# Experts by wide weight tiles, with 128 stationary columns and the second bias taken by gates

## The chip, the cores and the metric

One core of a Trainium2 chip runs the whole program: TensorE (PE, with its weight loads PEld), VectorE (DVE), ScalarE (ACT), GpSimd (POOL), SyncE (SP, which only issues DMAs here) and 16 DMA engines. The metric is device time in microseconds of one execution; before and after are compared by the median of runs.

## The reference, cut to what matters

Two transformer blocks over 512 tokens of width 1024. The change is in the mixture of experts that ends the first block: 32 experts, four for each token, so 64 tokens an expert on average.

```
logits = xt @ router_w + router_b
top_logit, top_idx = top_k(logits, 4)
gate = softmax(top_logit)
for each expert e, for the tokens that chose it:
    hid = x @ w1[e] + b1[e]                    # w1: 1024 x 2048
    glu = min(hid[:, :1024], 7)
    lin = clip(hid[:, 1024:], -7, 7)
    act = glu * sigmoid(1.702 * glu) * (lin + 1)
    y   = (act @ w2[e] + b2[e]) * gate         # w2: 1024 x 1024
out = x + gate2 * (sum of y over a token's experts)
```

All is fp32. The weights of the experts are 384 MiB, each read once.

## The kernel before, in words

**Products.** Each factor is cut into a high part (fp32r, a cast on ACT, L104) and a low part (a subtraction on DVE, L105), and a product is three matmuls: high x high, high x low, low x high (`mm3`, L98). For the experts the activations are stationary (96 places an expert, `CAP`) and the weights move, 512 columns a matmul.

**Weight tiles.** A tile of weights is 512 rows x 512 columns, 1 MiB, as [128, 4, 512]; an expert has twelve, eight of the first layer (L1) and four of the second (L2). `weights` (L968) writes the order: L1 of expert e, then L2 of expert e-1; at the end L1(30), L2(29), L2(30), L1(31), L2(31). SP loads tiles into eight raw buffers (`load`, L982); a load is issued when the tile that had its buffer is cut. The high and low parts have four buffers of a tile each, used by halves (`PB=2`: a cast and a subtraction for each half tile of 1024 elements a partition). `ahead` is 3: in step n of the loop the code issues the cut of tile n+3 (`split`), then the products of tile n, then whatever `plan` has hung behind step n (`after`). PE, ACT, DVE and SP keep this written order; each runs its own queue in order. GpSimd's order is the scheduler's.

**An expert.** With b the step of its first tile, `plan` (L1093) hangs: gather of the next expert's tokens (POOL, `gather` L1050) behind b; their transposes on PE (`turn` L1056) behind b+6 and the cut of these into xt (`parts` L1063: a copy on ACT, a subtraction on DVE, for each half of 384 elements) behind b+8. The hidden columns come as half 0 of gate and linear part (tiles b to b+3), then half 1. `swiglu` (L1071) runs behind b+4 and b+8 for 512 columns each: a min (DVE L1073), a silu (ACT), a clip (DVE L1076), a gating (DVE L1077). The gated rows (ln) are turned and cut into `at` behind b+11 to b+14. L2 of the expert begins at b+20; behind its last tile `finish` (L1137) multiplies y by gate and gate2 (ys, DVE L1134) and GpSimd adds the rows to `acc` in DRAM by a scatter (L1225).

**Biases.** b1 and b2 of all experts are held as high and low parts (`b1s`, `b2s`), cut in the first steps (`bias_split`, `BS`). A matmul with a one-hot column `e2` adds them: four for L1 and two for L2 of each expert.

**Around it.** `phase_r` (L748) makes the first residual, the router and the lists; `route` (L826) does a block of 128 tokens, with the gates in the tile B. `EARLY` tiles of weights are cut there with GpSimd doing the subtraction, and the third at the beginning of `phase_b`. The last expert isn't scattered: its rows (`last`, L1126) are put back by a one-hot matmul (`onehot`) while x gets `acc` by a DMA at step `SM` (L1180). Then `overflow` (a loop that usually runs no pass) and the norm of the second block.

Of the kernel before, what the change touches and what calls it, by code (L numbers as in the profile page):

```python
# [18 lines left out]
T = 512  # L19
# [15 lines left out]
SM = 378  # L35
YH = 2
F30 = 3
XN = 12
L30 = [8,8,9,9,10]
TS = 1  # L40
GO = 0
NG = 2
TQ = [("tr",2),("y",2)]
# [4 lines left out]
PB = 2  # L48
# [3 lines left out]
MB = dict(xg=1,xt=1,at=1,gl=2,ln=2,ys=1,raw=7,hl=4)  # L52
# [3 lines left out]
BS = [0,2,4,6,8,10]  # L56
LS = [7,5,6,8,9]
# [5 lines left out]
class Ker:  # L63
# [684 lines left out]
    def phase_r(self, RY, yH, yL):  # L748
# [10 lines left out]
        rowi = self.rowi = lp.tile([128, NT, 4], I32, name="rowi")  # L759
        self.ovr = lp.tile([1, 359], I32, name="ovr")  # L760
# [65 lines left out]
        def route(i, lg):  # L826
# [141 lines left out]
    def weights(self):  # L968

        L1 = lambda e: [(e, 1, hb, m, kh) for hb in range(2) for m in range(2) for kh in range(2)]  # L970
        L2 = lambda e: [(e, 2, kh, cb, 0) for kh in range(2) for cb in range(2)]
        seq = self.seq = []
        for e in range(NE):
            seq += L1(e) + (L2(e - 1) if e else [])
            if e == NE - 2:
                seq += L2(e)
        del seq[-4:]
        seq += L2(NE - 1)
        self.at_ = {c: n for n, c in enumerate(seq)}
        self.raw, self.hl = {}, {}  # L980

    def load(self, n):  # L982
        if n < len(self.seq):
            e, layer, u, v, kh = self.seq[n]
            if layer == 1:
                src = self.a["exp_w1"][0][e, 512 * kh:512 * kh + 512, 512 * u + D * v:512 * u + D * v + 512]
            else:
                src = self.a["exp_w2"][0][e, 512 * u:512 * u + 512, 512 * v:512 * v + 512]
            two = n % RAW >= self.nraw
            w = self.raw[n] = (self.wp2 if two else self.wp).tile([128, 4, 512], F32, name="wraw", tag="wraw",  # L990
                                                                  bufs=RAW - self.nraw if two else self.nraw)
            self.nc.sync.dma_start(w, src.rearrange("(k p) c -> p k c", p=128))
# [10 lines left out]
    def phase_b(self):  # L1003
# [8 lines left out]
        b2s = bb.tile([128, D], F32R, name="b2s")  # L1012
# [3 lines left out]
        for t in (b1s, b2s, e2):  # L1016
            nc.gpsimd.memset(t[64:128].bitcast(F32), 0.0)
# [4 lines left out]
        psum = self.pool(PS, "psb", space=PSUM)  # L1022
        P = lambda tag, bufs: psum.tile([128, 512], F32, name=tag, tag=tag, bufs=bufs)
        T_ = lambda tag, n=512: bp.tile([C, n], F32, name=tag, tag=tag, bufs=MB[tag])

        braw = {}

        def bias_load():
            for n, (src, c0, tag, w) in enumerate((("exp_b1", 0, "gl", 512), ("exp_b1", D, "gl", 512), ("exp_b1", 512, "ln", 512),
                                                   ("exp_b1", D + 512, "ln", 512), ("exp_b2", 0, "ys", 1024))):  # L1030
                t = T_(tag, w)
                for h in range(2):
                    nc.sync.dma_start(t[32 * h:32 * h + 32], a[src][0, :, c0:c0 + w])
                braw[n] = t, (b1s if n < 4 else b2s)[:, c0:c0 + w]
# [6 lines left out]
        def gate_rows():  # L1041
            for j in range(2):
                p = P("tr", 2)
                mm(p, self.ones[32 * j + 64:32 * j + 65, :], self.mod[2][32 * j + 64:32 * j + 65, :])
                nc.scalar.copy(g2[:, 512 * j:512 * j + 512], p[:C])
# [10 lines left out]
        def turn(src, b, c0):  # L1056

            p = P("tr", 2)
            for k in range(4):
                nc.tensor.transpose(p[:, k * C:(k + 1) * C], src[:, c0 + k * 128:c0 + (k + 1) * 128], self.ident[:C, :C])  # L1060
            return p[:, 0:4 * C].rearrange("p (k c) -> p k c", c=C), slice(4 * b, 4 * b + 4)

        def parts(t, dst, scale=1.0):  # L1063
            pv, ks = t
            self.act(dst[0][:, ks, :], pv, AF.Copy, scale=scale)
            nc.vector.scalar_tensor_tensor(dst[1][:, ks, :], pv, scale, dst[0][:, ks, :].bitcast(F32), op0=OP.mult, op1=OP.subtract)  # L1066
# [4 lines left out]
        def swiglu(pg, pl):  # L1071
            gl = T_("gl")
            nc.vector.tensor_scalar(gl, pg[:C], 7.0, None, op0=OP.min)  # L1073
# [4 lines left out]
            return ln  # L1078
# [14 lines left out]
        def plan(e):  # L1093

            b, y0 = at_[(e, 1, 0, 0, 0)], at_[(e, 2, 0, 0, 0)]
            if e + 1 < NE:
                after(b, keep(("xg", e + 1), lambda: gather(e + 1)))
                n = b + XN if e == NE - 2 else b + 6
                for q in range(2):
                    after(n, keep(("tx", e + 1, q), lambda q=q: turn(X["xg", e + 1], q, 512 * q)))  # L1100
                after(n + 1 if e == NE - 2 else max(min(at_[e + 1, 1, 0, 0, 0], b + 12) - ahead - 1, b + 7),
                      lambda: (X.__setitem__(("xt", e + 1), pair("at" if e == NE - 2 else "xt")),
                               [parts(X["tx", e + 1, q], X["xt", e + 1]) for q in range(2)]))
            steps = LS if e == NE - 1 else L30 if e == NE - 2 else (8, 11, 12, 13, 14)
            after(b + 4, keep(("ln", 0), lambda: swiglu(*X["hid", e, 0])))
            after(b + steps[0], keep(("ln", 1), lambda: swiglu(*X["hid", e, 1])))
            for q in range(2):
                after(b + steps[1 + 2 * q], keep(("t", q), lambda q=q: turn(X["ln", q], q, 0)))
                after(b + steps[2 + 2 * q], lambda q=q: (q or X.__setitem__(("at", e), pair("xt" if e >= NE - 2 else "at")),
                                                         parts(X["t", q], X["at", e], 1 / 1.702)))  # L1110
            if e < NE - 1:
                after(y0 + (F30 if e == NE - 2 else 4), lambda: finish(e))
            else:
                after(y0 + OH, onehot)
                for cb in range(2):
                    after(y0 + LA + cb, lambda cb=cb: last(cb))

        def onehot():

            io, t = T_("gl"), bp.tile([C, 1], F32, name="tlc")  # L1120
# [5 lines left out]
        def last(cb):  # L1126
            if cb == 0:
                X["ys"] = self.wp.tile([C, 4, 512], F32R, name="ysp", tag="wraw", bufs=self.nraw)
            ys = T_("ln")
            weigh(ys, NE - 1, cb)  # L1130
            self.split(X["ys"][:, cb], X["ys"][:, 2 + cb], ys)

        def weigh(ys, e, cb):
            nc.vector.scalar_tensor_tensor(ys, X["y", e][cb][:C], self.tlg[:, e:e + 1], g2[:, 512 * cb:512 * cb + 512],  # L1134
                                           op0=OP.mult, op1=OP.mult)

        def finish(e):  # L1137
            ys = T_("xg" if e == NE - 2 else "ys", D)
            for cb in range(2):
                weigh(ys[:, 512 * cb:512 * cb + 512], e, cb)  # L1140
            self.add_rows(ys, self.tli[:, e:e + 1])

        def products(n):
            e, layer, u, v, kh = seq[n]
            if layer == 1:
                if u == 0 and v == 0 and kh == 0:
                    plan(e)
                if v == 0 and kh == 0:
                    X["hid", e, u] = [P("hid", 4), P("hid", 4)]
                p, xt, bias = X["hid", e, u][v], X["xt", e], b1s[:, D * v + 512 * u:D * v + 512 * u + 512]  # L1150
            else:
                if u == 0 and v == 0:
                    X["y", e] = [P("hid", 4) if e >= NE - YH else P("y", 2) for _ in range(2)]
                p, xt, kh, bias = X["y", e][v], X["at", e], u, b2s[:, 512 * v:512 * v + 512]
            w = hl.pop(n)
            for k in range(4):
                kk = 4 * kh + k
                self.mm3(p[:C], (xt[0][:, kk, :], xt[1][:, kk, :]), w[k], kk == 0, False)
            if kh:
                mm(p[:C], e2[:, e:e + 1].to_broadcast([128, C]), bias, False, True)  # L1160

        ET_ = mybir.EngineType
        with self.tc.manual_schedule(engines={ET_.PE, ET_.Activation, ET_.DVE, ET_.SP}):
# [3 lines left out]
            for n in range(5):  # L1167
                after(BS[n], lambda n=n: bias_split(n))
            after(BS[5], gate_rows)
# [3 lines left out]
            for q in range(2):  # L1173
                parts(turn(X["xg", 0], q, 512 * q), X["xt", 0])
# [15 lines left out]
        ES.close()  # L1190
        self.overflow(P)
# [36 lines left out]
    def overflow(self, P):  # L1228
# [8 lines left out]
        with tc.For_i(0, n, 1) as b:  # L1237
# [27 lines left out]
            b1, b2 = (a[n_][0][bass.ds(e, 1), :] for n_ in ("exp_b1", "exp_b2"))  # L1265

            def gemm(xt, w, c0, bias):
                p = P("hid", 4)
                bb = op_.tile([1, 512], F32, name="bb", bufs=2)
# [561 lines left out]
```

## Time and profile before

| | us |
|---|---|
| runs of the kernel before, median of 3 | 2538.77 (2535.23 to 2539.68) |
| the profiled execution | 2528.63 |
| its span | 2526.8 |
| PE, DVE, ACT, POOL busy in it | 2432.6, 1837.4, 1378.7, 389.9 |
| PE matmuls into hid and y by lines, of 4512 | 1571.8 |
| DVE subtractions `wl` (L105), x974 | 1080.6 |

The profile is of one execution. Its times are microseconds from the start of the span; a name is a line of the kernel, an engine, an operation and the tiles written and read. Busy time counts overlapping instructions once, so the start-to-start distance of instructions in a row can be smaller than their duration. The experts run from about 531 to 1692 us, the second block after them.

### The profile page before, as it was taken

The page shows a single profiled execution, that of the slowest core. Times are in us where ns is not written, and L with a number is a line of the kernel's source. Part 1 is how long each engine was busy: PE and PEld are TensorE (multiplying, and loading weights), DVE is VectorE, ACT ScalarE, POOL GpSimd, SP SyncE. Part 2 cuts the span into 40 slices and gives each one's busy share as a digit, 9 for nine tenths or more (in the row PEclk, how much of TensorE's full clock was granted, in tenths as well). Part 3 has the DMA queues.
Part 4 walks back from the last instruction along what each step waited for, and adds up shares of the span by engine and source line. Part 5 has one row for each costly group of instructions (what it writes and reads, how often), then busy time and mean ns, then how long its engine had stood idle before and what let it go on. Part 6 is the DMA issues. An engine that isn't in the chain of part 4 may idle for free. (4 is left out here: it accounts for less than half of the span.)

```text
span 2526.8 us, 33228 instructions
## 1 busy us (share of the span) xinstructions
PE 2432.6 (96%) x12362; PEld 1785.6 (71%) x12362; DVE 1837.4 (73%) x2627; ACT 1378.7 (55%) x1956; POOL 389.9 (15%) x319
## 2 busy tenths in 40 slices
PE   6999998979999999999999999998999999899999
PEld 2677764756777777777777777667877678688887
DVE  3445566689999999999999999986765544555522
ACT  2433455357777777777777777764445543332221
POOL 2000223214221333233210111130100000000000
PEclk7999799989999999999999999998999999899999
DMA  9462100679999999999999999983411131433331
GB/s 277 151 199 67 50 1 30 231 250 337 349 375 370 369 374 375 371 370 369 367 368 366 369 373 372 373 250 103 94 51 42 43 89 63 119 96 99 93 100 67
DMA packets 371566, 556.75 MB, mean 220 GB/s; under 512 B 13138, under 2 KB 153501, under 8 KB 371401
## 3 DMA queue, kind: packets, MB, share of 16 engines
q1 hardware_dynamic: 359808, 518.81, 59.1%
q0 software_dynamic: 11120, 34.68, 6.0%
q8 instruction: 98, 1.61, 0.3%
q10 hardware_dynamic: 473, 1.11, 0.1%
q14 instruction: 67, 0.55, 0.1%
HBM read 534.06 MB, written 20.48 MB: 219 GB/s over the span
## 5 line engine op out<-in xcount | busy, mean ns | idle before, releaser
L105 DVE TENSOR_TENSOR wl<-wraw,wh 128x1024 fp32r<-128x1024 f32 (+2 forms) x974 | 1080.6, 1157 | 253.2 <-ACT wh L104 239.7
L104 ACT CAST wh<-wraw 128x1024 fp32r<-128x1024 f32 (+1 forms) x980 | 942.2, 998 | 542.8 <-PE mm L96 236.4
L96 PE MATMUL hid<-wh,xt 128*96 128x512 f32 x2048 | 671.4, 396 | 0.6 <-DVE xt L1066 0.5
L96 PEld LDWEIGHTS hid<-wh,xt 128*96 128x96 f32 x2048 | 331.5, 162 | 138.0 <-DVE xt L1066 1.2
L96 PE MATMUL hid<-wl,xt 128*96 128x512 f32 x1024 | 402.0, 393 | 0.0
L96 PE MATMUL y<-wh,at 128*96 128x512 f32 x960 | 310.0, 393 | 0.0
L1225 POOL DMA_INDIRECT acc<-ys,tli x30 | 190.6, 6353 | 545.1 <-DVE ys L1134 525.5
L96 PE MATMUL mm<-hH,wh 128*128 128x512 f32 x624 | 253.4, 407 | 3.3 <-ACT gate L1600 1.9
L96 PE MATMUL mm<-hL,wh 128*128 128x512 f32 x624 | 248.9, 399 | 0.0
L96 PE MATMUL mm<-hH,wl 128*128 128x512 f32 x624 | 248.7, 399 | 0.0
L96 PEld LDWEIGHTS hid<-wl,xt 128*96 128x96 f32 x1024 | 166.1, 162 | 63.9 <-issue 0.3
L96 PEld LDWEIGHTS y<-wh,at 128*96 128x96 f32 x960 | 155.4, 162 | 66.8
L96 PE MATMUL y<-wl,at 128*96 128x512 f32 x480 | 188.4, 393 | 0.0
L96 PEld LDWEIGHTS mm<-hH,wh 128*128 128x128 f32 x624 | 118.6, 190 | 37.3 <-issue 5.7
L96 PEld LDWEIGHTS mm<-hL,wh 128*128 128x128 f32 x624 | 118.4, 190 | 28.2 <-issue 3.8
L96 PEld LDWEIGHTS mm<-hH,wl 128*128 128x128 f32 x624 | 118.5, 190 | 27.1 <-issue 2.6
L74 ACT ACTIVATE gl<-gl 96x512 f32<-96x512 f32 x64 | 40.5, 632 | 156.9 <-DVE gl L1073 156.9
L96 PEld LDWEIGHTS y<-wl,at 128*96 128x96 f32 x480 | 77.6, 162 | 32.8
L1052 POOL DMA_INDIRECT xg<-h2d,tli x32 | 45.8, 1431 | 292.9 <-PE tr L1060 285.6
L96 PE MATMUL mu<-hH,wh 128*128 128x512 f32 x176 | 68.5, 389 | 0.0
L96 PE MATMUL mu<-hL,wh 128*128 128x512 f32 x176 | 68.5, 389 | 0.0
L96 PE MATMUL mu<-hH,wl 128*128 128x512 f32 x176 | 68.5, 389 | 0.0
(558 smaller groups left out, 3361.8 us busy)
## 6 DMA issues: line engine op xcount, KB each, us to landing
wraw<-in_exp_w_dram SPq DMA_DIRECT2D x384, 1024.0 KB
wraw<-in_w_in_dram SPq DMA_DIRECT2D x62, 512.0 KB
wraw<-in_ada_w_dram SPq DMA_DIRECT2D x48, 512.0 KB
wraw<-in_w_ffn_in_dram SPq DMA_DIRECT2D x44, 512.0 KB
wraw<-in_w_ffn_out_dram SPq DMA_DIRECT2D x22, 512.0 KB
wraw<-in_w_out_dram SPq DMA_DIRECT2D x4, 1024.0 KB
wraw<-in_w_o_dram SPq DMA_DIRECT2D x8, 512.0 KB
acc<-zf SPq DMA_DIRECT2D x1, 2432.0 KB
```

The lines of the kernel that those rows point to most:

```text
L74: ins = self.nc.scalar.activation(out, in_, func, **kw)
L96: self.nc.tensor.matmul(out, l, r, start=start, stop=stop, skip_group_check=True)
L104: self.nc.scalar.copy(h, src)
L105: (eng or self.nc.vector).tensor_sub(l, src, h.bitcast(F32))
L1052: self.gathered = nc.gpsimd.indirect_dma_start(out=xg, out_offset=None, in_=self.h2d, in_offset=bass.IndirectOffsetOnAxis(ap=self.tli[:, e ...
L1225: self.nc.gpsimd.indirect_dma_start(out=self.acc, out_offset=bass.IndirectOffsetOnAxis(ap=idx, axis=0), in_=ys, in_offset=None, compute_op ...
```

## The change

- A tile of an expert below 30 (`OLD`) becomes 256 rows x 1024 columns, [128, 2, 1024]; a tile of L1 is then wholly of the gate or of the linear part. Experts 30 and 31 keep the old tiles. Parts are cut by whole tiles (`PB=1`), 2048 elements a partition.
- The stationary factors xt and at have 128 columns, the last 32 zeroed once; the matmuls write all 128 rows.
- SwiGLU, the cuts of xt and at, ys and their PSUM tiles (`P2`, two banks) go by whole 1024 columns: min and silu behind b+4, clip behind b+8, gating behind b+9, turn behind b+11, cut of at behind b+12, cut of the next xt behind b+7.
- b2 leaves the products. The gates of each token by expert, G, are summed in `route` on GpSimd; b2 times gate2 is cut into `b3`, and in the last sums (x += one-hot @ rows) one more matmul adds G-turned @ b3.
- The gather leaves out places of index 512 and above (`bounds_check`); xg is zeroed once.
- At the end L2(30) comes between the halves of L1(31); `SM`, `LS`, `L30` and `BS` are moved.

```diff
-SM = 378
+SM = 379
-L30 = [8,8,9,9,10]
+L30 = [8,10,12,12,13]
+OLD = 30
-PB = 2
+PB = 1
-MB = dict(xg=1,xt=1,at=1,gl=2,ln=2,ys=1,raw=7,hl=4)
+MB = dict(xg=1,xt=1,at=1,gl=1,ln=1,ys=1)
-BS = [0,2,4,6,8,10]
-LS = [7,5,6,8,9]
+BS = [0,1,10,14]
+LS = [11,7,8,12,13]
...
+            nc.gpsimd.tensor_add(G[:, i, :], B[:, 0, NE:], B[:, 1, NE:])
+            for j in range(2, 4):
+                nc.gpsimd.tensor_add(G[:, i, :], G[:, i, :], B[:, j, NE:])
...
-            seq += L1(e) + (L2(e - 1) if e else [])
-            if e == NE - 2:
-                seq += L2(e)
-        del seq[-4:]
+            l1, l2 = L1(e), L2(e - 1) if e else []
+
+            seq += l1[:4] + l2 + l1[4:] if e == NE - 1 else l1 + l2
         seq += L2(NE - 1)
...
+            w = self.a["exp_w1" if layer == 1 else "exp_w2"][0][e]
+            if e < OLD:
+                v, kq = divmod(i, 4)
+                src, shape = w[256 * kq:256 * kq + 256, D * v:D * v + D], [128, 2, D]
...
+        def gated_bias():
+
+            t, _ = braw.pop(2)
+            nc.vector.tensor_mul(t, t, g2)
+            nc.scalar.copy(b3, t)
+            nc.vector.tensor_sub(b3[32:64], t[32:64], b3[32:64].bitcast(F32))
+
+        def turned_gates():
+
+            gb = X["gb"] = self.wp.tile([96, D + T], F32R, name="gb", tag="wraw", bufs=self.nraw)
+            G3 = self.wp.tile([128, 96 * NT], F32, name="G3", tag="wraw", bufs=self.nraw)
+            p, GT = P2("tr")[:, 0], gb[:, D:]
+            nc.gpsimd.tensor_copy(G3.rearrange("p (i r e) -> p i r e", r=3, e=NE), self.G.unsqueeze(2).to_broadcast([128, NT, 3, NE]))
+            nc.gpsimd.tensor_copy(gb[:, 0:D], b3)
+            for i in range(NT):
+                nc.tensor.transpose(p[:96, 128 * i:128 * i + 128], G3[:, 96 * i:96 * i + 96], self.ident)
+            nc.scalar.copy(GT, p[:96])
+            nc.vector.tensor_sub(GT[64:96], p[64:96], GT[64:96].bitcast(F32))
...
-            xg = T_("xg", D)
+            xg = T_("xg")
+            if e == 0:
+                nc.gpsimd.memset(xg, 0.0)
+
             self.gathered = nc.gpsimd.indirect_dma_start(out=xg, out_offset=None, in_=self.h2d,
-                                         in_offset=bass.IndirectOffsetOnAxis(ap=self.tli[:, e:e + 1], axis=0))
+                                         in_offset=bass.IndirectOffsetOnAxis(ap=self.tli[:, e:e + 1], axis=0),
+                                         bounds_check=T - 1, oob_is_err=False)
...
-            return [bp.tile([128, KD, 128], F32R, name=f"{name}{j}", bufs=MB[name])[:, :, 0:C] for j in range(2)]
+
+            if name not in X:
+                X[name] = [bp.tile([128, KD, 128], F32R, name=f"{name}{j}") for j in range(2)]
+                for t in X[name]:
+                    nc.gpsimd.memset(t[:, :, C:].bitcast(F32), 0.0)
+            return X[name]
...
+        def glu(gl, pg):
+            nc.vector.tensor_scalar(gl, flat(pg), 7.0, None, op0=OP.min)
             self.act(gl, gl, AF.Silu, scale=1.702)
-            ln = T_("ln")
-            nc.vector.tensor_scalar(ln, pl[:C], 7.0, -7.0, op0=OP.min, op1=OP.max)
+
+        def lin(ln, pl):
+            nc.vector.tensor_scalar(ln, flat(pl), 7.0, -7.0, op0=OP.min, op1=OP.max)
+
+        def gated(ln, gl):
             self.last = nc.vector.scalar_tensor_tensor(ln, ln, 1.0, gl, op0=OP.add, op1=OP.mult)
...
+                after(b + 6, keep(("tx", e + 1), lambda: turn(X["xg", e + 1], P2("tr"), 0, 2)))
+                after(b + 7,
+                      lambda: (X.__setitem__(("xt", e + 1), pair("xt")),
+                               parts(X["tx", e + 1], X["xt", e + 1], 0, 2)))
+            if e < OLD:
+                after(b + 4, lambda: (X.__setitem__("gl", T_("gl")), glu(X["gl"], X["hid", e, 0])))
+                after(b + 8, lambda: (X.__setitem__("ln", T_("ln")), lin(X["ln"], X["hid", e, 1])))
+                after(b + 9, lambda: gated(X["ln"], X["gl"]))
+                after(b + 11, keep("t", lambda: turn(X["ln"], P2("tr"), 0, 2)))
+                after(b + 12, lambda: (X.__setitem__(("at", e), pair("at")), parts(X["t"], X["at", e], 0, 2, 1 / 1.702)))
...
+            if e < OLD:
+
+                v, kq = divmod(i, 4)
+                todo_ = [(2 * kq + k, j, [t[:, 512 * j:512 * j + 512] for t in w[k]], D * v + 512 * j)
+                         for k in range(2) for j in range(2)]
...
+            for kk, j, wk, c0 in todo_:
+                self.mm3(p[:, j], (xt[0][:, kk, :], xt[1][:, kk, :]), wk, kk == 0, kk == KD - 1 and b0 is None)
+                if kk == KD - 1 and b0 is not None:
+                    mm(p[:C, j], e2[:, e:e + 1].to_broadcast([e2.shape[0], C]), b0[:, c0:c0 + 512], False, True)
...
+                mm(p, X["gb"][:, D + 128 * i:D + 128 * i + 128], X["gb"][:, cs], True, False)
                 for j in range(2):
-                    mm(p, X["one"][:, 128 * i:128 * i + 128], X["ys"][:, 2 * j + cb], j == 0, j == 1)
+                    mm(p, X["one"][:, 128 * i:128 * i + 128], X["ys"][:, 2 * j + cb], False, j == 1)
```

## Rows read from the trace of the kernel before

**Rows 1.** A stretch of the expert stage: length, engines' busy time (instructions), clock, DMA share, GB/s.

```profile
820.00:1590.00 770.00, 770.00 (x3565) 546.45 (x3564) 737.85 (x769) 569.73 (x640) 181.35 (x44) 1.00 1.05 370
```

**Rows 2.** Timeline of GpSimd: start, duration, line, operation; gathers (xg) and scatters (acc).

```profile
655.89 1.15 POOL L1052 DMA_INDIRECT xg<-h2d,tli  x1 [6.50 <-PE tr L1060]
...
1249.31 2.63 POOL L1225 DMA_INDIRECT acc<-ys,tli  x1 [17.74 <-DVE ys L1134]
...
1576.85 6.35 POOL L1225 DMA_INDIRECT acc<-ys,tli  x1 [22.52 <-DVE ys L1134]
1588.94 1.92 POOL L1052 DMA_INDIRECT xg<-h2d,tli  x1 [5.74 <-PE tr L1060]
```

**Rows 3.** Timeline of PE among the experts, and the chain's piece of the final projection.

```profile
999.83 0.62 PE L96 MATMUL hid<-wh,xt 128*96 128x512 f32 x2
...
1009.73 0.62 PE L96 MATMUL hid<-wh,xt 128*96 128x512 f32 x2
...
2402.43 119.69 PE ro L96 x528
```

**Rows 4.** Timeline of DVE over one expert while it catches up.

```profile
699.15 1.02 DVE L1066 SCALAR_TENSOR_TENSOR xt<-tr,xt 128x384 fp32r<-128x384 f32 x2
700.09 0.68 DVE L1073 TENSOR_SCALAR gl<-hid 96x512 f32<-96x512 f32 x1
700.68 0.68 DVE L1076 TENSOR_SCALAR ln<-hid 96x512 f32<-96x512 f32 x1
...
702.40 9.17 DVE L105 TENSOR_TENSOR wl<-wraw,wh 128x1024 fp32r<-128x1024 f32 x8 [0.25 <-ACT wh L104]
711.49 1.40 DVE L1134 SCALAR_TENSOR_TENSOR ys<-y,tlg,g2b 96x512 f32<-96x512 f32 x2
712.82 0.54 DVE L1066 SCALAR_TENSOR_TENSOR at<-tr,at 128x384 fp32r<-128x384 f32 x1
...
734.23 1.01 DVE L1066 SCALAR_TENSOR_TENSOR xt<-tr,xt 128x384 fp32r<-128x384 f32 x2
```

**Rows 5.** Waits, us in total, times, longest: 900 to 1300, then 1250 to 1600.

```profile
ACT wh L104 <- DMA wraw<-in_exp_w_dram: 8.9, 15, 1.4
...
ACT wh L104 <- DMA wraw<-in_exp_w_dram: 40.5, 68, 1.7
```

**Rows 6.** DMA totals of two stretches of 2 us: 458 to 460, then 452 to 454.

```profile
DMA packets 391, 0.77 MB, mean 385 GB/s; under 512 B 15, under 2 KB 15, under 8 KB 391
...
DMA packets 200, 0.82 MB, mean 412 GB/s; under 512 B 0, under 2 KB 0, under 8 KB 199
```

**Rows 7.** Forms of splits on DVE and ACT (xcount, busy, mean ns), and ACT beside a SwiGLU.

```profile
L105 DVE TENSOR_TENSOR wl<-wraw,wh 128x1024 fp32r<-128x1024 f32 x862 | 1005.1, 1219 | 174.6 <-ACT wh L104 161.4 <-PE st L96 8.5 <-issue 0.2
...
L105 DVE TENSOR_TENSOR aL<-ft,aH 128x512 fp32r<-128x512 f32 x22 | 15.1, 685 | 0.0
...
L104 ACT CAST wh<-wraw 128x1024 fp32r<-128x1024 f32 x868 | 875.6, 1049 | 426.2 <-PE mm L96 153.5 <-PE ro L96 83.0 <-PE hid L96 79.4
L104 ACT CAST wh<-wraw 128x512 fp32r<-128x512 f32 x104 | 63.5, 619 | 114.4 <-PE mm L96 80.8 <-PE ro L96 19.9 <-issue 8.7
...
1021.21 0.63 ACT L74 ACTIVATE gl<-gl 96x512 f32<-96x512 f32 x1 [2.06 <-DVE gl L1073]
1021.75 6.77 ACT L104 CAST wh<-wraw 128x1024 fp32r<-128x1024 f32 x7
```

**Rows 8.** Timelines of DVE, PE and GpSimd at the start and end of the stage.

```profile
532.83 2.36 DVE L105 TENSOR_TENSOR wl<-wraw,wh 128x1024 fp32r<-128x1024 f32 x2 [0.38 <-ACT wh L104]
...
1636.99 0.88 PE L1060 MATMUL tr<-ident,ln 96*128 96x96 f32 x4 [4.24 <-DVE ln L1077]
...
1676.62 2.60 POOL L1180 DMA_DIRECT2D x<-acc  x2
...
1691.89 0.40 PE L96 MATMUL hid<-b2s,e 128*96 128x512 f32 x1
...
1694.67 7.03 PE L96 MATMUL hid<-ysp,one 96*128 96x512 f32 x16 [2.38 <-issue]
```

More of the change, by code (lines that the diff above doesn't have):

```diff
@@ L759, in phase_r @@
         rowi = self.rowi = lp.tile([128, NT, 4], I32, name="rowi")
+        G = self.G = lp.tile([128, NT, NE], F32, name="G")
         self.ovr = lp.tile([1, 359], I32, name="ovr")
@@ L1011, in phase_b @@
         b1s = bb.tile([128, 2 * D], F32R, name="b1s")
-        b2s = bb.tile([128, D], F32R, name="b2s")
+        b3 = bb.tile([96, D], F32R, name="b3")
         e2 = bb.tile([128, NE], F32R, name="e2")
         bb.tile([128, 24], F32, name="pad")
-        for t in (b1s, b2s, e2):
+        for t in (b1s, e2):
             nc.gpsimd.memset(t[64:128].bitcast(F32), 0.0)
@@ L1093, in plan @@
         def plan(e):
-            b, y0 = at_[(e, 1, 0, 0, 0)], at_[(e, 2, 0, 0, 0)]
+            b, y0 = at_[(e, 1, 0)], at_[(e, 2, 0)]
             if e + 1 < NE:
                 after(b, keep(("xg", e + 1), lambda: gather(e + 1)))
-                n = b + XN if e == NE - 2 else b + 6
-                for q in range(2):
[L1100 to L1110, printed above, removed]
+                after(b + 6, keep(("tx", e + 1), lambda: turn(X["xg", e + 1], P2("tr"), 0, 2)))
@@ L1114, in plan @@
                 after(y0 + OH, onehot)
+                after(y0 + 2, turned_gates)
                 for cb in range(2):
@@ L1141, in finish @@
             self.add_rows(ys, self.tli[:, e:e + 1])
         def products(n):
[L1144 removed]
+            e, layer, i = seq[n]
             if layer == 1:
[L1146 removed]
+                if i == 0:
                     plan(e)
[L1148 to L1154 removed]
+                if i % 4 == 0:
+                    X["hid", e, i // 4] = P2("hid")
+                p, xt, b0 = X["hid", e, i // 4], X["xt", e], b1s
+            else:
+                if i == 0:
+                    X["y", e] = P2("hid" if e >= NE - YH else "y")
+                p, xt, b0 = X["y", e], X["at", e], None
@@ L1155, in products @@
             w = hl.pop(n)
[L1156 to L1160, printed above, removed]
+            if e < OLD:
+                v, kq = divmod(i, 4)
+                todo_ = [(2 * kq + k, j, [t[:, 512 * j:512 * j + 512] for t in w[k]], D * v + 512 * j)
+                         for k in range(2) for j in range(2)]
+            else:
+                u, j, kh = (i // 4, i // 2 % 2, i % 2) if layer == 1 else (0, i % 2, i // 2)
+                todo_ = [(4 * kh + k, j, w[k], 512 * u + D * j if layer == 1 else 512 * j) for k in range(4)]
@@ L1166, in phase_b @@
             bias_load()
-            for n in range(5):
+            for n in range(2):
                 after(BS[n], lambda n=n: bias_split(n))
-            after(BS[5], gate_rows)
+            after(BS[2], gate_rows)
+            after(BS[3], gated_bias)
             X["xg", 0], X["xt", 0] = gather(0), pair("xt")
@@ L1172, in phase_b @@
                 split(n, nc.gpsimd)
-            for q in range(2):
-                parts(turn(X["xg", 0], q, 512 * q), X["xt", 0])
+            parts(turn(X["xg", 0], P2("tr"), 0, 2), X["xt", 0], 0, 2)
             for n in range(len(seq)):
@@ L1190, in phase_b @@
         ES.close()
+        PP.close()
+        psum = self.pool(PS, "psb", space=PSUM)
+        P = lambda tag, bufs: psum.tile([128, 512], F32, name=tag, tag=tag, bufs=bufs)
         self.overflow(P)
@@ L1263, in trans, with gemm @@
                 return t
-            b1, b2 = (a[n_][0][bass.ds(e, 1), :] for n_ in ("exp_b1", "exp_b2"))
-            def gemm(xt, w, c0, bias):
+            b1 = a["exp_b1"][0][bass.ds(e, 1), :]
+            def gemm(xt, w, c0, bias=None):
                 p = P("hid", 4)
-                bb = op_.tile([1, 512], F32, name="bb", bufs=2)
-                nc.sync.dma_start(bb, bias)
-                mm(p[:C], self.ones[0:1, 0:C], bb, True, False)
+                if bias is not None:
+                    bb = op_.tile([1, 512], F32, name="bb", bufs=2)
+                    nc.sync.dma_start(bb, bias)
+                    mm(p[:C], self.ones[0:1, 0:C], bb, True, False)
                 for k in range(KD):
```

102 lines of the change are left out of this document (56 added, 46 removed).

## The prediction

> **What bounds the kernel now.** The page has TensorE (PE) busy for 96% of the span, so I read the expert stage by itself, and looked for who waits there. By one such stretch [rows 1] PE has no idle time at all from 820 to 1590 us, VectorE (DVE) is busy for 96% of it and the DMA engines are full. The GpSimd timeline gives the pace: the gather that follows PE's transposes goes from 655.89 to 1588.94 in 26 experts, 35.887 us each [rows 2]. That is PE's own pace: 43 matmuls with 96 stationary columns take 9.90 us, 230.2 ns each [rows 3]; 150 x 0.2302 = 34.53, and the 1.36 that are left go to two groups of eight transposes.
>
> Two engines stand close behind. DVE: in the stretch where it had fallen behind and was catching up, it repeats itself every 35.08 us (699.15 to 734.23) [rows 4]. Start to start: 24 halves of a weight tile at 1.135, two pairs of parts (xt, at) 0.93 each, one pair of ys 1.33, two SwiGLU groups 2.31 each; sum 35.05. DMA: in the early window ScalarE (ACT) waited for weights 8.9 us of 400, late 40.5 of 350 [rows 5]; over those nine late experts the scatter that follows DVE slips from 1249.31 to 1576.85, 36.39 each, while PE still runs at 35.887 [rows 2]. So the weights come at about 36.4 us an expert and live on a lead won early.
>
> **The change, part by part.**
>
> PE. Stationary 128 instead of 96 columns: the final projections, the same form (activations stationary, 512 moving columns), take 119.69 / 528 = 226.7 ns [rows 3]. Six bias matmuls an expert become four. 148 x 0.2267 + 1.36 = 34.91 us, 0.98 less. If 128 columns should give nothing: 148 x 0.2302 + 1.36 = 35.43.
>
> DMA. A tile of 256 rows x 1024 columns has runs of 4 KB instead of 2 KB. Before the stage both kinds pass: 391 packets of mostly 2 KB in 2 us at 385 GB/s, 200 packets of mostly 4 KB (x) at 412 [rows 6]. Twelve tiles are 12.58 MB: 32.7 us against 30.5. The gather brings on average 64 of 96 places (512 tokens x 4 / 32 experts), 0.13 MB less, 0.3 us. So 36.4 - 2.2 - 0.3 = 33.9; bounds 33.9 to 36.1 (runs without effect). The order of scatter and gather stays.
>
> The page "DMA: Bandwidth & Descriptors" of the Trainium skill (section "Where 436 GB/s comes from") says that loads from HBM are bound by about 358 GB/s a core. The stage before already moves 370 on average [rows 1], so the trace does not agree; as a rival it comes below.
>
> DVE, the part that decides. One subtraction takes a whole tile. The same line takes 685 ns on 512 elements and 1219 on 1024 [rows 7], 1.043 ns an element; so of 1.135 us start to start 0.067 are fixed, and 2048 elements take 2.20, between 2.13 (nothing fixed) and 2.27 (two halves). I take 2.20: 26.4 us an expert. xt and at by one instruction each: 0.93 - 0.07 = 0.86, twice. ys 1.33 - 0.13 = 1.20. The lin clip 0.60 + 0.53 = 1.13; the gating 1.14.
>
> The first step, the min for the gate half, is not just its 1.21 us. Code order on DVE: subtraction of tile b+7, min, subtraction of tile b+8; on ACT: cast of b+7, silu, cast of b+8. The silu must wait for the min, the cast of b+8 for the silu, the subtraction for the cast: DVE stands still for silu and cast, however far ACT is ahead. Before, this was hidden: the other clip and the gating filled the time of a half-wide silu, and the next cast was half a tile (0.25 us were left [rows 4]). Now clip and gating are moved to b+8 and b+9 and nothing fills it. Sizes: a silu 0.54 start to start at 512 elements [rows 7], with the slope of the casts (1049 - 619 ns for 512 [rows 7]) 0.96 at 1024; a cast 1.05 + 0.86 = 1.91; the min 0.68 + 0.53 = 1.21 [rows 4] and 0.03 to hand over. From min to next subtraction 1.24 + 0.96 + 1.91 = 4.11 us, of which 2.9 are idle. Followed in the same way, the other moved steps find no wait: at b+7 and b+12 ACT's copy of xt or at runs beside a subtraction; clip and gating have their inputs long before.
>
> DVE's new cycle: 26.4 + 0.86 + 0.86 + 1.20 + 1.13 + 1.14 + 4.11 = 35.7 us. Ends: 34.9 and 36.5 by the two prices of a subtraction. PE's 34.91 and the weights' 33.9 lie below. So the bound changes from PE at 35.89 to DVE at 35.7. PE will idle 0.8 us an expert, where its transposes of the gated rows (after b+11) wait for the gating: subtraction of b+12 and gating lie ahead of it on DVE. What is late next is PE.
>
> The page "VectorE: DVE Perf Modes" of the Trainium skill (section "The TRN2 errata") speaks for more: the fixed cost is paid once an instruction, for a two-input fp32 operation 151 cycles, an estimate of 1.9 us an expert for twelve instructions less. The row's 1.135 start to start leaves room for 0.067 each, so the trace does not bear it out; by that rule the cycle would be 34.6 and PE the bound, the first rival.
>
> The whole stage. DVE's first own tile began at 532.83, PE's last matmul at 1691.89, ending at 1692.3 [rows 8]. After: start at 533.7 (a whole cast ahead). 32 x 35.7 = 1143 us, less three tiles that GpSimd cuts (6.6) and the first xt and last ys (2.1), plus the first biases (five wide operations in place of four narrow and a wide one, 4.9 in all), some 20 tiny operations of the overflow list (3) and waits for PE at the start (2.5, an estimate): 1145, to 1679. Then PE does two tiles and four transposes of the gates (5.9): 1685, 7 us earlier. In it is PE's 4.24 us stall before its transposes at 1636.99 [rows 8], which goes since the layer that needed them now follows half of the last expert.
>
> Against it, at the ends. Before the stage the gate table is summed by 12 small GpSimd additions between routing steps and GpSimd's subtractions are twice as long (each can hold up small DVE operations): +1, between 0 and 3. After it the second bias is 8 more matmuls among 16 that take 7.03 us [rows 8], 0.44 each, the first ones under the wait for ys: +2, between 0 and 3.5. The last-but-one scatter comes four tiles later than now, and the accumulated rows are fetched behind it (now issued at 1676.62 [rows 8]): the fetch loses most of its cover; +1, between 0 and 5. The zeroing of xg and the pads replaces that of b2s, nothing. GpSimd's queue: the fetch waits for the scatter in front of the copies that turned_gates needs, if they stand behind it; that is in the 5.
>
> Sum: -7 + 1 + 2 + 1 = -3, 2528.6 to about 2525.5 for the profiled execution. The median of the runs shown, 2538.8, is 10.1 us longer than that execution. The trace cannot say where. The weights are the part without reserve: the lead that covers 0.5 us an expert was nearly used up, and weights slower by 1% would cost some 10 us before, and none after. I give 4 of the 10 to that: 2538.8 - 3 - 4 = about 2532.
>
> **The rivals.**
> 1. DVE does not hold PE back (cycle under 34.9). For it: PE's gain is sure from a row of the same form. Against: 2.9 us of idle follow from code order alone. Then 32 x 0.98 = 31 us go, less 4 at the ends: 2512.
> 2. Slower: the wait behind min costs more than wide operations save. The place is the same one; it decides from a cycle of 36.0 on, which is a subtraction of 2.23 us, between my 2.20 and two halves. At 36.5 the stage takes 32 x 0.8 = 26 us more than in my sum, 2558; at 36.1 2545. Before-rows speak for a fixed part that is saved, so the near end is likelier.
> 3. The weights stay the bound: long runs give nothing beside scatters and gathers, and at 36.1 an expert (above) the lead of before is soon gone. Stage 32 x 0.4 = 13 us over my sum, 2545. The 412 beside 385 [rows 6] speak against it. By the page's 358 GB/s the 13.16 MB of an expert would be 36.8 us and the time, an estimate, about 2563.
> 4. The longer matmul row gives nothing: PE at 35.43 is still under DVE; 2533. A rival in the reason, not in the time.
>
> **How the numbers follow.** What a measurement of this kernel can tell from no change is about 0.2%, 5 us. My case (DVE's cycle 35.4 to 36.0) has 0.58 with a range of 2522 to 2542; of it 0.33 are faster, 0.23 same, 0.02 slower. Rival 1: 0.16, faster. Rival 2: 0.18, of it 0.05 same. Rival 3: 0.03. Rival 4: 0.05, same. Faster 0.49, same 0.33, slower 0.18. Range 2509 to 2547.
>
> **What would show it.** Matmuls 227 ns apart, gathers 35.7 apart, PE idle nearly 0.8 us an expert at its transposes with DVE's gating as releaser; DVE idle 2.9 us once an expert with the cast as releaser; no wait of ACT for weights. Wrong: PE without idle time and 34.9 an expert; or DVE's subtraction far from 2.2 us; or ACT waiting for DMA.

## The result and the profile after

The changed kernel takes 2549.29 us (median of 7 runs, 2548.00 to 2558.86) against 2538.77 (7 runs, 2528.21 to 2553.51): ratio 1.0058, 95% interval 1.0030 to 1.0086. It is slower. The prediction said 2532 and not above 2547.

The two profiled executions take 2557.01 us (span 2555.2) and 2528.63. The first is among the longest of its seven runs, the second at the short end of its own, so I compare by stretches. The index list (tli) ends the routing; gathers are numbered from 1 to 32.

| us | before | after | difference |
|---|---|---|---|
| start to the index list | 522.8 | 533.0 | +10.2 |
| list to gather 1 | 3.0 | 4.3 | +1.3 |
| gather 1 to 6 | 130.1 | 139.8 | +9.7 |
| gather 6 to 32 | 933.0 | 931.1 | -2.0 |
| gather 32 to the second block's first transposes | 118.3 | 132.0 | +13.8 |
| from there to the end | 819.6 | 815.0 | -4.6 |

The first line is hardly the change: 8.1 of it are there at one instruction of GpSimd, before and after, up to which both kernels run the same code:

```profile
435.63 0.17 POOL L802 IOTA tid<- 128x16 int32 x1 [7.48 <-PE pm L96]
```

```profile
443.75 0.17 POOL L804 IOTA tid<- 128x16 int32 x1 [7.48 <-PE pm L96]
```

Windows of the kernel before, then after, 360 to 400 us (length, busy time of PE, its weight loads, DVE, ACT, GpSimd, with counts; granted clock, DMA share, GB/s):

```profile
360.00:400.00 40.00, 39.62 (x308) 27.44 (x306) 22.90 (x48) 23.64 (x55) 11.05 (x19) 1.00 0.01 1
```

```profile
360.00:400.00 40.00, 39.62 (x277) 27.48 (x275) 21.12 (x43) 20.06 (x47) 10.64 (x18) 0.85 0.00 1
```

PE is equally busy and does 277 matmuls in place of 308: the granted clock is 0.85 of 2.4 GHz over the window, so part of it ran at the lower level, 1.2 GHz, although PE had been busy for 39.5 of the 40 us before, at 1.00. The other 2 us of the line are the change's: from that instruction to the list it is 87.2 and 87.3 us in the two kernels with the old routing (before, before_128) and 88.8 to 90.7 in the eleven with the new one. It is not the sums of the gates: no_gates, without them, has 88.8.

From the list to the end the change costs 2022.2 - 2004.0 = 18.2 us in these two executions. Up to the second block it is 22.8. The last line is code that the change hardly touches, and the thirteen profiles have anything from 811.6 to 819.6 us there.

The steady stage is what was predicted. One stretch, the gathers, and PE among the experts, of the changed kernel:

```profile
820.00:1590.00 770.00, 757.93 (x3530) 620.97 (x3528) 708.23 (x388) 537.58 (x325) 53.70 (x43) 1.00 1.01 370
```

```profile
677.05 1.01 POOL L1085 DMA_INDIRECT xg<-h2d,tli  x1 [2.35 <-PE tr L1093]
713.14 0.98 POOL L1085 DMA_INDIRECT xg<-h2d,tli  x1 [11.99 <-PE tr L1093]
...
1608.13 0.98 POOL L1085 DMA_INDIRECT xg<-h2d,tli  x1 [12.03 <-PE tr L1093]
```

```profile
1002.34 0.39 PE L96 MATMUL y<-wh,at 128*128 128x512 f32 x1
...
1010.97 0.61 PE L96 MATMUL y<-wh,at 128*128 128x512 f32 x2
```

(1608.13 - 713.14) / 25 = 35.80 us an expert against 35.89 [rows 2]; 38 matmuls in 8.63 us are 227 ns against 230 [rows 3]; PE, never idle in [rows 1], now idles 12.07 us of 770, 0.56 an expert (I had 0.8). DVE over one cycle, and waits from 900 to 1300 us (total, times, longest), of the changed kernel, beside [rows 4, 5]:

```profile
1007.03 2.28 DVE L105 TENSOR_TENSOR wl<-wraw,wh 128x2048 fp32r<-128x2048 f32 x1
...
1013.70 6.68 DVE L105 TENSOR_TENSOR wl<-wraw,wh 128x2048 fp32r<-128x2048 f32 x3
1020.31 1.27 DVE L1192 SCALAR_TENSOR_TENSOR ys<-y,tlg,g2b 96x1024 f32<-96x1024 f32 x1
...
1031.18 1.21 DVE L1114 TENSOR_SCALAR gl<-hid 96x1024 f32<-96x1024 f32 x1
1035.30 2.35 DVE L105 TENSOR_TENSOR wl<-wraw,wh 128x2048 fp32r<-128x2048 f32 x1 [2.92 <-ACT wh L104]
```

```profile
ACT gl L74 <- DVE gl L1114: 49.5, 11, 4.5
...
DVE wl L105 <- ACT wh L104: 32.1, 11, 2.9
...
PE tr L1093 <- DVE ln L1121: 6.0, 11, 0.6
```

Three subtractions take 1020.31 - 1013.70 = 6.61, 2.20 each. After the min DVE waits 2.92 us, once an expert, for the cast behind the silu. ACT waits nowhere for weights.

The end is another matter. PE's stalls behind gather 32 in the changed kernel, where the kernel before has 4.24 and 2.38 [rows 8] and, ahead of the second block, 5.50 us (first fence):

```profile
1707.19 1.12 PE L1371 MATMUL y<-ident,xn 128*128 128x128 f32 x4 [5.50 <-DVE xn L1367]
```

```profile
1666.43 0.90 PE L1093 MATMUL tr<-ident,ln 96*128 96x96 f32 x4 [5.46 <-DVE at L1101]
1704.36 0.55 PE L1093 MATMUL tr<-ident,ln 96*128 96x96 f32 x4 [0.95 <-DVE ovr L1301]
1713.43 0.64 PE L1073 MATMUL tr<-ident,G 128*96 128x128 f32 x4 [2.62 <-POOL G L1070]
1716.24 0.79 PE L96 MATMUL hid<-wh,at 128*128 128x512 f32 x1 [2.17 <-DVE ln L1192]
...
1726.45 0.79 PE L96 MATMUL hid<-gb 96*128 96x512 f32 x1 [5.85 <-DMA ng<-in_norm_g_dram]
...
1740.16 1.11 PE L1439 MATMUL y<-ident,xn 128*128 128x128 f32 x4 [5.03 <-DVE xn L1435]
```

### The profile page after: what moved, and what is told of

Same layout as the page of the kernel before. It is cut to its first block, busy times and chain, and to the rows that moved or that the text cites. A ratio compares the mean times of both kernels' runs of the same rounds, so it can differ in the third digit from the quotient of the medians.

```text
span 2555.2 us, 31728 instructions
## 1 busy us (share of the span) xinstructions
PE 2427.1 (95%) x12310; PEld 1905.3 (75%) x12310; DVE 1784.4 (70%) x2059; ACT 1322.1 (52%) x1474; POOL 265.8 (10%) x334
## 4 chain that ended last, share of the span: by engine, by line
PE 56%; DVE 11%; issue 8%; DMA 2%; ACT 2%; DVEq 0%; POOL 0%; ACTq 0%; SPq 0%; POOLq 0%
PE hid L96 24%; PE mm L96 15%; DVE wl L105 7%; PE ro L96 6%; PE mu L96 5%; PE s L96 2%; PE po L96 1%; DVE ln L1121 1%; DVE ln L1118 1%; ACT wh L104 1%; DVE xt L1101 1%; PE tr L1093 1%; PE pt L1721 1%; DMA acc<-xg,tli 1%; DMA x<-acc 1%
## 5 line engine op out<-in xcount | busy, mean ns | idle before, releaser
L105 DVE TENSOR_TENSOR wl<-wraw,wh 128x2048 fp32r<-128x2048 f32 (+3 forms) x589 | 1050.0, 1812 | 315.0 <-ACT wh L104 302.8
L104 ACT CAST wh<-wraw 128x2048 fp32r<-128x2048 f32 (+3 forms) x592 | 894.6, 1529 | 609.2 <-PE mm L96 232.0
L96 PE MATMUL hid<-wh,xt 128*128 128x512 f32 x2048 | 670.6, 396 | 3.9 <-DVE xt L1101 2.5
L96 PEld LDWEIGHTS hid<-wh,xt 128*128 128x128 f32 x2048 | 388.5, 190 | 88.7 <-DVE xt L1101 2.9
L96 PE MATMUL hid<-wl,xt 128*128 128x512 f32 x1024 | 402.4, 393 | 1.9 <-DVE wl L105 1.9
L96 PE MATMUL y<-wh,at 128*128 128x512 f32 x960 | 301.0, 389 | 0.0
L96 PEld LDWEIGHTS hid<-wl,xt 128*128 128x128 f32 x1024 | 194.5, 190 | 41.8 <-DVE wl L105 2.3
L96 PEld LDWEIGHTS y<-wh,at 128*128 128x128 f32 x960 | 180.2, 188 | 38.6
L96 PE MATMUL y<-wl,at 128*128 128x512 f32 x480 | 187.2, 390 | 1.4 <-DVE wl L105 1.4
L96 PEld LDWEIGHTS mm<-hH,wh 128*128 128x128 f32 x624 | 118.3, 190 | 36.1 <-issue 5.1
L1292 POOL DMA_INDIRECT acc<-ys,tli x30 | 52.7, 1758 | 609.8 <-DVE ys L1192 609.2
```

The source lines that it names most:

```text
L96: self.nc.tensor.matmul(out, l, r, start=start, stop=stop, skip_group_check=True)
L104: self.nc.scalar.copy(h, src)
L105: (eng or self.nc.vector).tensor_sub(l, src, h.bitcast(F32))
L1292: self.nc.gpsimd.indirect_dma_start(out=self.acc, out_offset=bass.IndirectOffsetOnAxis(ap=idx, axis=0), in_=ys, in_offset=None, compute_op ...
```

## The experiments

Each run's ratio is to the kernel before on the same chip. "List to end" is the part of the profiled span behind the index list (before 2004.0, after 2022.2), which leaves the early clock out.

**The wait in VectorE's order.** The silu goes one step later; it then stands behind the next cast:

```diff
-after(b + 4, lambda: (..., glu(X["gl"], X["hid", e, 0])))    # min, silu
+after(b + 4, lambda: (..., X.__setitem__("silu", glu(...))))  # min
+after(b + 5, lambda: X["silu"]())                             # silu
```

> The changed kernel with one move: ScalarE's silu of a wide tile comes one step later, behind the next weight cast, so that VectorE's minimum and its wait for the next cast no longer follow each other. Theory A (VectorE's order sets the stage: 32.9 us of work and one wait of 2.9 us make its cycle of 35.8 us, and any VectorE work added in the first experts is paid in full): the wait goes, TensorE becomes the bound at 34.9 to 35.2 us per expert, scatters stand 35.0 to 35.2 apart, and the time falls by 15 to 25 us, 2525 to 2534. Theory B (weights set the 35.8 us: 12.6 MB per expert at 351 GB/s): the period stays at 35.7 to 35.8 and the time within 3 us of 2549.

Measured: 2534.79 (2514.41 to 2549.15), ratio 0.9994 (0.9967 to 1.0020); list to end 1987.7, 34.5 less than after. A stretch, two gathers, and waits from 900 to 1300 us:

```profile
820.00:1590.00 770.00, 770.00 (x3602) 635.89 (x3601) 724.53 (x395) 556.38 (x330) 233.71 (x44) 1.00 1.02 378
```

```profile
800.13 2.13 POOL L1085 DMA_INDIRECT xg<-h2d,tli  x1 [6.56 <-PE tr L1093]
...
1571.74 2.13 POOL L1085 DMA_INDIRECT xg<-h2d,tli  x1 [6.57 <-PE tr L1093]
```

```profile
DVE wl L105 <- ACT wh L104: 24.8, 36, 0.8
...
ACT gl L74 <- DVE gl L1114: 6.2, 12, 0.5
```

771.61 / 22 = 35.07 us an expert, PE without idle time: theory A, to the size in the period; the time lies just above its 2525 to 2534. The longest wait falls from 2.92 to 0.8. Gather 1 to 6 falls from 139.8 to 130.7 as well: PE's stalls of 2.50, 1.36, 1.72, 1.90 and 0.85 us there become 1.57 and 1.49. So the wait cost twice, 0.73 an expert in the steady stage and several us among the first experts, where DVE also carries the biases and the overflow list. The second gain can be lost again: in silu_cols96, gates_early, code_pad and best1, which have the later silu too, the stretch takes 139.8 to 142.0, since DVE waits 7.5 to 8.4 us there for the first scatter (gates_early below shows it). The pair best2 and ends_only, further down, settles its size.

Weights keep up, theory B falls. The weights' own DMA queue in silu_late, from 820 to 1590 us (packets, MB, share), then from 660 to 760, and in the kernel before from 820 to 1590:

```profile
q1 hardware_dynamic: 73656, 276.07, 93.9%
```

```profile
q1 hardware_dynamic: 9598, 37.00, 94.1%
```

```profile
q1 hardware_dynamic: 134675, 267.47, 94.9%
```

The 378 GB/s above counts all queues; the weights alone move 276.07 MB in 770 us, 358.5 GB/s, and from 660 to 760 us 370. The 358 GB/s of the Trainium skill, "DMA: Bandwidth & Descriptors" (section "Where 436 GB/s comes from"), which that section gives as what binds loads from HBM, is reached here by one core's weights over the stage and passed in the shorter stretch.

**128 columns**, undone in the changed kernel (cols96, the edit below) and with the later silu (silu_cols96), and put alone into the kernel before (before_128):

```diff
-self.mm3(p[:, j], (xt[0][:, kk, :], xt[1][:, kk, :]), wk, ...)
+self.mm3(p[:C, j], (xt[0][:, kk, 0:C], xt[1][:, kk, 0:C]), wk, ...)
```

> The changed kernel with 96 stationary columns in place of 128 in the experts' products. Theory A (VectorE's order sets the period): TensorE goes back to 230 ns a product, 35.4 us per expert, still under 35.8: the period stays at 35.8 and the time within 3 us of 2549. Rival E (TensorE sets the period, its idle 1.6% being the tail of its own queue): 35.8 goes to 36.3 and the time to 2560 to 2566.

> The run silu_late (silu one step later, 35.07 us per expert, TensorE the bound) with 96 stationary columns in place of 128. If 128 columns give what the prediction took (230.2 to 226.7 ns a product, 144 products), the period rises by 0.4 to 0.5 us, to 35.4 to 35.6, and the time by 10 to 14 us over silu_late. Rival (128 columns give nothing, the gain of silu_late is the wait alone): the period stays at 35.07 and the time within 3 us.

> The kernel before with 128 stationary columns alone. There TensorE sets the period (35.89 us, VectorE 35.05). From silu_cols96 against silu_late (35.400 and 35.073) 128 columns take 0.33 us off an expert, 10 us off the 32: the period falls to 35.5 to 35.6 and the time to 2527 to 2531. Rival (VectorE's 35.05 and weights leave no room): within 3 us of the kernel before.

Measured: 2560.10, ratio 1.0074 (1.0045 to 1.0103), period 35.75, list to end 2020.2; 2547.61, ratio 1.0030 (0.9998 to 1.0062), period 35.40; 2531.59, ratio 0.9972 (0.9947 to 0.9997). In the changed kernel the columns are worth nothing by stretches. The median, 11 us up, lies in rival E's range, but the ratio's interval overlaps the changed kernel's (1.0030 to 1.0086), and the period speaks against E. With the wait gone they are worth 35.40 - 35.07 = 0.33 an expert; two gathers of silu_cols96, 25 experts apart:

```profile
712.92 2.03 POOL L1085 DMA_INDIRECT xg<-h2d,tli  x1 [9.04 <-PE tr L1093]
...
1597.91 2.03 POOL L1085 DMA_INDIRECT xg<-h2d,tli  x1 [9.09 <-PE tr L1093]
```

Alone in the kernel before they give it 35.67 in most experts, and 37.1 to 37.9 in three late ones: there the weights are late (ACT waits 64.8 us for them from 820 to 1520), with the tiles still narrow. My 35.5 to 35.6 was too low for that.

**The end: the order of the last experts.** The second layer of expert 30 ahead of expert 31, with its steps (`L30`, `LS`, `SM`) as before:

```diff
-seq += l1[:4] + l2 + l1[4:] if e == NE - 1 else l1 + l2
+seq += l1 if e == NE - 1 else l1 + l2 + (L2(e) if e == NE - 2 else [])
```

> The changed kernel with the order of the last two experts as before the change: the second layer of expert 30 ahead of expert 31's first layer, the two turned tiles swapping places as before, the steps L30, LS and SM as before. Theory C (about 12 us are lost at the stage's end because the scatter of expert 30, now half an expert later, holds the fetch of the sum, which holds GpSimd's copies for the last product): the scatter is issued about 12 us earlier, the fetch no longer waits for it, the second block begins 8 to 13 us sooner, the time is 2536 to 2542. Rival D (the end is set by TensorE's own 16 steps of the last experts, and the fetch is hidden): within 3 us of 2549.

Measured: 2550.64, ratio 1.0068 (1.0043 to 1.0093). The fetch is issued 83.8 us behind gather 32 in place of 99.9, and the second block begins 127.9 behind it in place of 132.0. The chain of the changed kernel runs through scatter and fetch, and yet 16 us off them give 4: theory C falls. What is late next are the stalls above: PE waits 5.66 us for the turned rows, 2.17 behind the gates and 5.31 ahead of the last product.

**The end and the second bias.** Left out altogether, then with its copies and transposes earlier (both on the places of the diff; the second with the later silu):

```diff
-after(BS[3], gated_bias)       # no_gates: also G, the load, the product
...
-after(y0 + 2, turned_gates)
+after(373, turned_gates)       # gates_early: GpSimd's copies
+after(374, turn_gates)         # TensorE's transposes
```

> The changed kernel without the second bias: neither its load, its product with the gate row, GpSimd's sums of the gates, the turned gates, nor the last product with them (this part of the result is left out). It bounds what the part 'second bias by gates' costs outside the steady stage. By my count 1 to 3 us at the routing and up to 6 us at the end (GpSimd's two copies of 1.5 us behind the fetch and TensorE's transposes behind these) and 3 us of VectorE in the first experts: 2539 to 2546. Rival (the end waits for the fetch anyway, and the rest is hidden): within 2 us of 2549.

> silu_late with the two copies of the turned gates (GpSimd) and TensorE's four transposes nine and eight steps earlier, ahead of the last-but-one scatter and of the fetch of the sum in GpSimd's queue. If TensorE's stalls at these transposes (2.4 and 2.2 us in silu_late) come from that queue alone, both go, and the stretch from the last gather to the second block (129.3 us in silu_late) falls by 3 to 5 us. Rival (the stage's end waits for the fetch of the sum, issued 97 us after the last gather): the stalls go and the wait ahead of the last product grows by as much, 128 to 130 us.

Measured: 2549.85, ratio 1.0061 (1.0028 to 1.0094), list to end 2016.6, so 5.6 less by stretches (3.8 less among the first experts and 4.1 behind gather 32, 2.3 more elsewhere); the median is the rival's, and I call it undecided. 2544.90, ratio 1.0006 (0.9971 to 1.0041). In gates_early the stall at the gates moves (3.91 us, at an earlier place), the one behind it shrinks to 0.84, and gather 32 to the second block takes 129.2 as in silu_late: the rival. Its early experts took 139.8 in place of 130.7. DVE there:

```profile
643.38 4.47 DVE L105 TENSOR_TENSOR wl<-wraw,wh 128x2048 fp32r<-128x2048 f32 x2
655.53 1.28 DVE L1197 SCALAR_TENSOR_TENSOR ys<-y,tlg,g2b 96x1024 f32<-96x1024 f32 x1 [7.68 <-DMA acc<-ys,tli]
```

The first scatter stood behind sixteen token-list transfers on GpSimd, which took 58 us (0.97 to 9.63 each); DVE waited 7.68 for it, PE 8.01. In silu_late, with the same code up to there, they took 52 and DVE waited 1.16.

**The gap ahead of the last product.** 24 small matmuls ahead of the first expert, added to silu_late (gap 5.47), move all TensorE code behind them:

```diff
+for _ in range(24):
+    mm(t0[:, 0, 0:8], self.ones[64:65, :], self.mod[2][64:65, 0:8])
```

> silu_late with 24 matmuls of 8 columns put into TensorE's idle time ahead of the first expert; they move all later TensorE code by about a fifth of a 16 KB instruction packet. In the changed kernel two such packets are fetched one after the other behind the last expert (1722.4 and 1725.6 us) and TensorE goes on 0.8 us behind the second; in the kernel before it is one. If the place of the packets' borders is what costs there, the gap ahead of the last product falls from 5.5 us to about 2.4 us. Rival (the gap is the wait for the fetch of the sum or the loop's branch itself): it stays at 5 to 6 us.

Measured: 2536.25, ratio 0.9993 (0.9960 to 1.0025). DMA totals from 1721 to 1727 us of the changed kernel, then the same place of code_pad, 1702 to 1706, and PE there:

```profile
q8 instruction: 2, 0.03, 2.0%
```

```profile
q8 instruction: 1, 0.02, 2.1%
```

```profile
1704.90 0.80 PE L96 MATMUL hid<-gb 96*128 96x512 f32 x1 [2.31 <-issue]
```

The gap is 2.31 us, as in the kernel before (2.38, one packet on that queue), and gather 32 to the second block takes 126.6 for 129.2. The changed kernel fetched two packets of 16 KB one after the other behind the overflow loop, which is left by a branch; PE went on 0.83 us after the second began. All thirteen profiles agree in this: the five with one packet (before, before_128, code_pad, best2, ends_only) have a gap of 2.28 to 2.38 us, the eight with two have 5.31 to 8.33 (the 8.33 is no_gates, where the fetch of the sum lands 1.1 us before PE goes on). So the releaser that the view names (DMA ng) is a neighbour in time. That PE waits for just the second packet is likely and not shown: in best1 it went on 0.12 us before that one began. The Trainium skill, "Runtime: NRT & Kernel Launch" (section "Instruction fetch mechanics"), says that a taken branch to code outside the present window waits for a fetch; the trace agrees in that a fetch stands in every one of these gaps, and a second one goes with some 3.2 us more.

**Together.** best1 is the later silu with gates early, the memsets behind the first gather, and the second layer of expert 30 behind two steps of expert 31; best2 adds the pad and the token lists in four groups, with the rest of the overflow list behind them; ends_only is best2 without the later silu.

```diff
+self.order(nc.gpsimd.memset(...), self.gathered)   # pads, b1s, e2
-seq += l1[:4] + l2 + l1[4:] if e == NE - 1 else l1 + l2
+seq += l1[:2] + l2 + l1[2:] if e == NE - 1 else l1 + l2
-L30 = [8,10,12,12,13]; LS = [11,7,8,12,13]; YH = 2; SM = 379
+L30 = [8,10,11,12,13]; LS = [11,9,10,12,13]; YH = 1; SM = 376
-after(b + 4, lambda: swiglu(e, 0))
+after(b + (8 if e == NE - 1 else 4), lambda: swiglu(e, 0))
+if n in (30, 42, 54, 66): self.token_lists((n - 30) // 12, lists)
```

> silu_late with all that the traces point to: GpSimd's seven memsets (4 us) behind the first gather, the second layer of expert 30 behind two steps of expert 31 in place of four, with its halves turned in steps of their own, and the turned gates early. Against silu_late the first gather comes 2.5 to 3 us sooner behind the index list, the stalls of 4.5 and 4.6 us at the end go, and the sum's fetch starts 5 to 6 us sooner: 8 to 13 us less, 2520 to 2527 where silu_late had 2535. Rival (the half-clock stretches and the fetch take back what the stalls give): within 4 us of silu_late.

> best1 with two more edits: the 24 small matmuls of code_pad, and GpSimd's sixteen transfers of the token lists in four groups of four over four experts in place of sixteen in a row. In best1 and gates_early the sixteen take 58 us, the first scatter stands behind them, VectorE waits 7.7 us for it and TensorE 8 us, with 6.8 us at the half clock behind that. Expected: the stretch from the first to the sixth gather falls from 140.5 to 127 to 132 us, the gap ahead of the last product from 5.5 to 2.4 us, and the time by 10 to 16 us, to 2512 to 2519. Rival (the token lists only hid another wait): the stretch stays above 137 us and the time at 2522 to 2528.

> best2 without the later silu, so the changed kernel with its start and its end mended and VectorE's wait left in. Steady period 35.8 as in the changed kernel. If the ends and the wait are two separate losses, the stretch from the last gather to the second block falls from 132.1 to 117 to 120 us, index list to first gather from 4.3 to 1.5 us, the early experts stay slow (136 to 140 us), and the time is 2530 to 2536: all that the ends cost, 13 to 19 us, and no more. Rival (the end's stalls were only the shadow of the wait): 2540 or more.

| | median (range), us | ratio (95%) | list to gather 1 | 1 to 6 | 32 to block 2 | list to end |
|---|---|---|---|---|---|---|
| best1 | 2528.50 (2512.31 to 2550.28) | 0.9939 (0.9903 to 0.9975) | 1.55 | 140.5 | 119.8 | 1986.3 |
| best2 | 2512.46 (2504.41 to 2519.49) | 0.9898 (0.9867 to 0.9929) | 1.55 | 132.4 | 115.0 | 1978.6 |
| ends_only | 2548.54 (2535.92 to 2559.89) | 1.0026 (1.0000 to 1.0052) | 1.55 | 139.7 | 119.2 | 2011.9 |

best2 (6 runs) beats both kernels and falls into its forecast; best1 lies 1.5 us above its own, with its first experts at 140.5. best2 and ends_only differ in nothing but the step of the silu, on the same chip: 36.1 us by medians, 33.3 from list to end, 7.3 of these from gather 1 to 6. That is the wait by itself. In the two rows below, the first is of best1, the second is best2's first product behind the loop:

```profile
1646.42 0.55 PE L1094 MATMUL tr<-ident,ln 96*128 96x96 f32 x4 [1.08 <-DVE at L1102]
```

```profile
1676.20 0.50 PE L96 MATMUL hid<-gb 96*128 96x512 f32 x1 [2.31 <-issue]
```

The stall of 5.46 us goes to 1.08 in best1, which among its other edits turns the halves in steps of their own (ends_only has 2.06 there). In best2 the token lists no longer hold the scatter, 8.1 us, although the small matmuls stretch gather 1 to 2 from 7.0 to 10.5. In ends_only the stretches named in its forecast came out as expected, 10.3 us from list to end, but the median is its rival's (2540 or more); the ends are worth 10 to 13 us by stretches, about 8 by the ratios to the kernel before (1.0026 for 1.0058). One expert of it took 39.62 us, with DVE's tiny operations of the overflow list (4.17 us) in it; with PE as the bound, in best2, the same place took 36.83 and the next expert 34.43. The bound engine hides nothing. The gathers around that expert in ends_only:

```profile
786.19 0.98 POOL L1087 DMA_INDIRECT xg<-h2d,tli  x1 [12.01 <-PE tr L1095]
825.81 1.01 POOL L1087 DMA_INDIRECT xg<-h2d,tli  x1 [1.74 <-PE tr L1095]
```

## Why the prediction was wrong

- **PE, right.** 227 ns a matmul. Where PE is the bound an expert takes 35.07, I had 34.91; against 96 columns that is 0.33, I had 0.52.
- **Weights, right.** No wait at 35.80, nor at 35.07. Rival 3 falls. But the 370 GB/s of [rows 1], which I held against 358, counts all queues: the weights alone moved 267.47 MB in 770 us there, 347 GB/s, so it was no evidence. And the time by 358 GB/s comes to some 2566 by my own sum, not 2563.
- **DVE's cycle, right.** 35.80 for 35.7, with a subtraction of 2.20 and the idle 2.92 for 2.9 behind min, silu and cast. silu_late shows that this wait alone kept 0.73 us an expert from PE. Rivals 1 and 2 (under 34.9, over 36.0) did not come.
- **"The whole stage": the step that failed.** I multiplied that cycle by 32 and had PE end 7 us earlier; from the list to PE's last product of expert 31 it took 18.1 us more (1187.6 for 1169.5). DVE began its own tiles 2.6 us later behind the list (12.6 for 10.0) rather than 0.9: 1.3 by GpSimd's memsets ahead of the first gather, 1.3 by the longer cuts of the first tiles. From the start of its first to the end of its last own tile it took 1162.1 us, where I had 1145 (the terms add up to 1144). Its first 33 tiles took 118.8, some 10 over the cycle and my extras (silu_late has 110.8, best2 105.1); the last dozen took 43.0 in place of 35.7. The narrow steps there have the min, silu, cast of their own, but that wait is 1.1 us each; the larger part, 5.0, is DVE behind ACT's cast, which waited behind the stall of PE in the next point. ACT, then DVE:

```profile
1672.11 1.91 ACT L104 CAST wh<-wraw 128x2048 fp32r<-128x2048 f32 x1 [4.26 <-PE hid L96]
```

```profile
1674.06 2.29 DVE L105 TENSOR_TENSOR wl<-wraw,wh 128x2048 fp32r<-128x2048 f32 x1 [5.02 <-ACT wh L104]
```

  The 27 dozens between add 2.6, by 35.80 for 35.7.
- **"PE's 4.24 us stall goes".** It came back as 5.46: the second half is turned into the same PSUM tile that DVE still reads (the releaser is DVE at). best1, with these steps moved, has 1.08.
- **"Then PE does two tiles and four transposes, 5.9".** It took 12.9, with 4.8 at the gates' transposes: GpSimd's copies stood behind the fetch, as I had noted and put into a +1. gates_early shows that moving them to the step ahead of the transposes gives nothing: the stall is 3.91 there, at the earlier place. best1 leaves two steps between copies and transposes, and has 1.12.
- **The ends, +4.** Mis-sized: behind expert 31's last product I had +3; to block 2 it took 19.6 us for 14.9, 3.2 more with the second instruction packet, which I had not thought of (code_pad), and 1.7 by the 8 products more (8.7 for 7.0). Ahead of the stage I had +1 and it was some 2.
- **The 10 us between profile and median, of which I gave 4 to weights,** need not be weights, and no run shows the 4. In the thirteen profiles the instruction shown at 435.63 us comes anywhere from 433.2 to 449.7 behind the same code; where before and after part, it is in a stretch at the lower clock, as in the windows above. How often each kernel falls into it stays open, since one execution of each was profiled. With it stays open whether the change costs 10 us (medians) or 18 to 23 behind the list (stretches).

## What to carry to other kernels

A steady cycle times its count is not the stage. An engine made the bound with little room left pays in full for all that only single rounds carry, the first and last above all, so those have to be walked instruction by instruction. If a wide operation joins two engines in a chain (min, silu, next cast), put the other engine's link one step later. And the chain of waits names what ended last, not what follows close behind: 16 us off it were worth 4.

## What was not expected of the hardware

- Behind a branch, TensorE's code came in two 16 KB packets in a row in eight profiles and in one in five, and with two it stood still some 3 us longer; 24 matmuls more in front changed two into one.
- Sixteen equal indirect transfers from GpSimd beside a full weight stream took 30 us in the kernel before, 42 in the changed kernel and 58 in gates_early (0.97 to 9.63 each there), with nothing changed about them.
- Two executions of the same early code differ by 8 us; the difference comes in one stretch at a lower granted clock of TensorE (0.85 and 1.00 in one window), with TensorE as busy as before it.
